# Context outputs of an S5 layer in quarters of TensorE, a later turn of the modulation, and other places for the first pages

## The chip, the core and the metric
One core of one Trainium2 chip. The metric is the device time of one launch, in microseconds (us). TensorE is called PE, VectorE DVE, ScalarE ACT, GpSimd POOL and SyncE SP, as in the profile; SP only issues DMAs here. TensorE's clock has two levels, 1.2 and 2.4 GHz; the profile gives it as a share of the upper one, so 0.50 is 1.2 GHz.

## What is computed
One inference step of a hybrid diffusion backbone, two layers deep: layer 0 mixes tokens with a bidirectional S5 state-space model, layer 1 with attention, and each is followed by a SwiGLU FFN. There are 256 context tokens and 1024 latent tokens of width 1024. All is fp32. The change lies in layer 0. Cut to what matters:

```python
def adaln(cvec, w_mod, b_mod):                  # the modulation
    m = jax.nn.silu(cvec) @ w_mod + b_mod
    return jnp.split(m[:, None, :], 6, axis=-1)

# s5_mixer: u = h @ w_in, 64 groups of 16 channels, each with a 64-dim complex state
...
s_re, s_im = scan(ab, bu)                       # per direction
y = einsum('blgp,ghp->blgh', s_re, c_re) - einsum('blgp,ghp->blgh', s_im, c_im)
...
z = jax.nn.gelu(y.reshape(b, l, D_MODEL))       # y also has d_skip * u
val, gate = jnp.split(z @ w_glu, 2, axis=-1)
return (val * jax.nn.sigmoid(gate)) @ w_out, finals
```

Context tokens and latent tokens go through the same mixer, each with its own modulation and its own initial states; the final states of the context are an output too.

## The kernel before
**Scan in blocks.** The S5 layer (`mixer0`) treats eight tokens as one block: 128 blocks for the latents, 32 for the context. The states at the block borders are found by a scan on DVE over two tiles X0 and X1 (32 groups of channels each; columns 0 to 128 hold the latents' states, 129 to 161 the context's). Inside a block, outputs come from tables: for each group a table of three 128x128 matrices multiplies the real part of the border states, their imaginary part, and the block's inputs U. The groups are handled in eight lots of eight (`fb`); the tables of a lot are one tile `tt` of 1.5 MB, loaded from DRAM (`s5_out_load`, L591, three buffers).

**Context outputs.** `ctx_items` (L636) yields the context's work in pieces. `states(fb)` copies a lot's border states out of X on ACT (L646, L647). `out(fb, h)` does half a lot: for each of four groups one matmul with the table's U part (L665) and two with its state parts (L667), the table as weights and 32 columns moving; a program-level fp32 matmul is two instructions. After the second half come a Gelu (L669), a store of the result to the DRAM buffer dZC on the POOL queue (L670), the load of the table three lots later, the states of two lots later, and `zload` of the lot before (L683, POOL queue), which brings dZC back turned into the tile zc. Then `net(t, h)` multiplies zc by the GLU weights (L698; loads L690 on SP), with a sigmoid or a copy on ACT (L704, L707), a product on POOL (L708) and a store (L709).

**Latents.** `s5_states` (L607) copies a lot's states, half on DVE (L614) and half on ACT (L617), or both on ACT (L616). `s5_out` (L620) has the same matmuls with 128 columns (L629, L631), a Gelu (L632) and a store of Z to dZL on POOL (L633). Between the latents' outputs stand pieces of `ctx_items`. Nine GLU products stand before the first latent output in the order of the program.

**Order.** In `mixer0` every engine runs its instructions as they are written. The function `drive` decides how the scan and the pieces are interleaved by a small clock of its own, from the number that each piece yields. Behind the mixer, in `rest`, only SP and POOL keep the written order; a planner places the instructions of PE, DVE and ACT. Memory pages are handed out in the written order of the program.

**Front of the FFN-like part.** `rest` starts with 16 page loads that bring dZL back turned (`zload` in `rest`, L1738 to L1742: two column chunks c, eight kt each), the splits into a high and a low part (L953 on ACT, L954 on DVE), and the weight loads and their splits (`i_load` L1028, `i_step` L1053, L1058, L1062). Products are L1100, 12 matmuls each. The pages used first lie over X1, whose last reader is the states of lot 7.

**Modulation.** 20 of the products of the conditioning with `w_mod` (`gemv`) are left; most are done in the mixer, the last 12 in `rest` by `gemv_next` (L201), once per piece of work: load four half pages (`hp`, L220, on ACT's queue), multiply a quarter that was loaded three calls earlier (L210), and after the fourth quarter copy the sum to a page (L214), turn it with four small products (L184, `gemv_tr`) and write it away (`gemv_fin`, L195, L196).

Of the kernel before, what the change touches and what calls it, by code (L numbers as in the profile page):

```python
# [6 lines left out]
F32 = mybir.dt.float32  # L7
F32R = mybir.dt.float32r
I32 = mybir.dt.int32
AF = mybir.ActivationFunctionType  # L10
# [3 lines left out]
P = 128  # L14
D = 1024
KT = 8
# [6 lines left out]
NG = 64  # L23
# [5 lines left out]
class Kernel:  # L29
# [171 lines left out]
    def gemv_next(self):  # L201

        nc = self.nc
        if len(self.gv) == 3 or not self.todo and self.gv:
            l, b, z, t = self.gv.pop(0)
            if z == 0:
                self.gp = self.psum()
            h, a = z // 2, z % 2
            for q in range(4):
                nc.tensor.matmul(self.gp[32 * q:32 * q + 32, 256 * h:256 * h + 256], self.sS[:, 4 * a + q, :], t[q],  # L210
                                 start=(a == 0), stop=(a == 1), tile_position=(0, 32 * q), skip_group_check=True)
            if z == 3:
                s = self.page()
                nc.scalar.activation(s, self.gp, AF.Copy)  # L214
                self.gemv_fin(l, b, self.gemv_tr(s))
        if self.todo:
            l, b, z = self.todo.pop(0)
            t = [self.half() for _ in range(4)]
            for q in range(4):
                nc.scalar.dma_start(t[q], self.I["w_mod"][l, b, :, 4 * (z % 2) + q, 256 * (z // 2):256 * (z // 2) + 256])  # L220
            self.gv.append((l, b, z, t))

# [9 lines left out]
class S5(Kernel):  # L232
# [355 lines left out]
                v.tensor_tensor(nxt, w[:, 0], w[:, 1], op=ALU.add)  # L588
                yield t + m * H / 960

    def s5_out_load(self, fb, ctx=False):  # L591

        nc = self.nc
        t = self.upool.tile([P, 8, 3, 128], F32, tag="tt", bufs=3, name=self.nm("tt"))
        nc.sync.dma_start(t, self.dW[:, fb])
        if ctx:
            U = [self.Uc[:, 8 * fb + k, :] for k in range(8)]
        else:

# [36 lines left out]
    def ctx_items(self):  # L636
# [2 lines left out]
        ld, W = [], []  # L639
        sc = {}  # L640

        def states(fb):
            X = self.X[fb // 4]
            gs = slice(8 * (fb % 4), 8 * (fb % 4) + 8)
            S = sc[fb] = sc["x"][:, fb % 2, 0:512].rearrange("p (g r c) -> p g r c", g=8, r=2)
            nc.scalar.activation(S[0:64], X[0:64, gs, :, 129:161], AF.Copy)  # L646
            nc.scalar.activation(S[64:128], X[64:128, gs, :, 160:128:-1], AF.Copy)  # L647

        def begin():
            ld.extend(self.s5_out_load(fb, True) for fb in range(3))  # L650
# [6 lines left out]
        def out(fb, h):  # L657
            U, t = ld[fb]
            if h == 0:
                sc["Z"] = sc["x"][:, fb % 2, 512:768]  # L660
                sc["ps"] = self.psum()
            ps = sc["ps"]
            for k in range(4 * h, 4 * h + 4):
                o = ps[:, 32 * k:32 * k + 32]
                nc.tensor.matmul(o, t[:, k, 2, :], U[k], start=True, stop=False)  # L665
                for ri in range(2):
                    nc.tensor.matmul(o, t[:, k, ri, :], sc[fb][:, k, ri, :], start=False, stop=(ri == 1))  # L667
            if h:
                nc.scalar.activation(sc["Z"], ps[:, 0:256], AF.Gelu_apprx_tanh)  # L669
                nc.gpsimd.dma_start(self.dZC[fb].rearrange("(p g) c -> p g c", g=8),  # L670
                                    sc["Z"].rearrange("p (g c) -> p g c", g=8))
                if fb < 5:
                    ld.append(self.s5_out_load(fb + 3, True))
                else:
                    self.ld.append(self.s5_out_load(fb - 5))
                if fb < 6:
                    states(fb + 2)
                if fb in (1, 3):
                    load()
                if fb:  # L680
                    zload(fb - 1)

        def zload(kt):  # L683
            nc.gpsimd.dma_start(self.zc[:, kt].rearrange("p (j c) -> p j c", j=8),
                                self.dZC[kt].rearrange("(j q) c -> q j c", j=8))
# [4 lines left out]
                nc.sync.dma_start(r, self.I["w_s5_glu"][len(W)])  # L690
                W.append(r)

        def net(t, h, ks=range(KT)):
            if ks[0] == 0:
                sc["ps", t, h] = self.psum()[:, 0:256]
            ps = sc["ps", t, h]
            for k in ks:
                nc.tensor.matmul(ps, W[2 * t + h][:, P * k:P * k + P], self.zc[:, k, :], start=(k == 0), stop=(k == KT - 1))  # L698
            if ks[-1] < KT - 1:
# [13 lines left out]
            for h in range(2):  # L713
                yield 2.6, lambda: out(fb, h)

        yield 2.6, lambda: net(0, 0, range(6))
        yield 3.5, lambda: (zload(7), net(0, 1, range(6)))
        for h in range(2):
            yield 0.9, lambda: net(0, h, range(6, 8))
        for t in range(1, 8):  # L720
            for h in range(2):
                yield 3.5, lambda: net(t, h)
# [937 lines left out]
class Full(Attn):  # L1660
# [40 lines left out]
    def rest(self):  # L1701
# [40 lines left out]
                                  self.dZL[kt].rearrange("(j q) c -> q j c", j=8)[:, 4 * c:4 * c + 4])  # L1742

        self.x_start(zz)
        for c in (0, 1):
            zload(c)
        self.x_all("B11", "B21")
        rest, k = self.x_rest("T1", "T2", "T3", "T4", "B22"), 0
        for c, units in self.ffn_heads(AF.Sigmoid):
            for u in units:  # L1750
                u()
                k += 1
                for _ in range(2 if k > 2 else 0):
                    next(rest, None)
                for _ in range(GN if k > GK else 0):
                    self.gemv_next()
        self.out_start(KT, TWO, self.spilled)
# [81 lines left out]
    def mixer0(self):  # L1839
# [182 lines left out]
        g, sm, tp = [self.gemv_load(*todo[0])], {}, {}  # L2022
        gk = [0]
        self.todo, self.gv = [(l, b, z) for l, b in todo[NGV:] for z in range(4)], []

        def gemv_step():
            k = gk[0]
# [209 lines left out]
```

## Time and profile before
| | us |
|---|---|
| median of 3 runs | 3416.73 |
| lowest and highest | 3413.44, 3417.08 |
| the profiled run | 3412.01 |
| its span, first to last instruction | 3410.2 |
| PE busy in it | 3254.1 (95%) |
| DVE busy | 2036.1 (60%) |
| ACT busy | 1390.3 (41%) |
| PE's share of the chain of waits that ended last | 76% |

The profile is that of one execution. The chain of waits is followed back from the last instruction, each step to what released it. "Idle before" is the time an engine sat idle ahead of an instruction, with what ended that idle time behind an arrow. PEld is the load of weights, which can run beside matmuls.

### The profile page before, as it was taken

What the parts mean: (1) busy time and instruction counts of PE and PEld (TensorE: products, weight loads), DVE (VectorE), ACT (ScalarE), POOL (GpSimd) and SP (SyncE); (2) the same over time, 40 slices, a digit from 0 to 9 for tenths busy, and PEclk for the clock granted to TensorE, in tenths of its full rate; (3) what the DMA queues carried; (4) which work ended last, traced back from release to release, by engine and by line L of the source; (5) the groups of instructions that cost most, each with busy time, mean ns of one, the idle gap of its engine ahead of it and who ended that gap; (6) DMA issues with size and microseconds to landing.
All of it is one profiled execution on the core that took longest, in us unless ns stands there. A gap on an engine that the chain in (4) does not pass through costs nothing.

```text
span 3410.2 us, 48179 instructions
## 1 busy us (share of the span) xinstructions
PE 3254.1 (95%) x18262; PEld 2759.6 (81%) x18262; DVE 2036.1 (60%) x4279; ACT 1390.3 (41%) x2714; POOL 287.6 (8%) x326
## 2 busy tenths in 40 slices
PE   8989979998999999999999999999889999999997
PEld 5768866677778888888788899999777888888787
DVE  8789716455574444443665788887557444444545
ACT  3261243243533222332544477775353322233433
POOL 2331100011000000001012310000100000000000
PEclk9996889999899999999999999999989999999998
DMA  7676675652231222343432200002123222235544
GB/s 257 177 227 237 209 251 183 192 201 74 86 102 66 69 67 73 118 150 106 145 115 76 68 24 11 14 27 75 68 88 98 69 70 72 69 105 192 173 127 146
DMA packets 204056, 398.81 MB, mean 117 GB/s; under 512 B 22624, under 2 KB 95616, under 8 KB 201520
## 3 DMA queue, kind: packets, MB, share of 16 engines
q1 hardware_dynamic: 154128, 322.52, 29.1%
q10 hardware_dynamic: 41040, 45.76, 4.0%
q0 software_dynamic: 8656, 27.45, 2.5%
q8 instruction: 143, 2.34, 0.3%
q14 instruction: 89, 0.73, 0.1%
HBM read 314.91 MB, written 84.93 MB: 117 GB/s over the span
## 4 chain that ended last, share of the span: by engine, by line
PE 76%; DVE 5%; ACT 3%; DMA 2%; issue 1%; ACTq 0%; SPq 0%; POOL 0%; DVEq 0%; POOLq 0%
PE ps L1100 29%; PE ps L121 9%; PE ps L123 8%; PE ps L125 8%; PE ps L1110 7%; PE ps L1549 2%; PE ps L1570 1%; PE ps L1569 1%; PE ps L1568 1%; PE ps L1507 1%; PE ps L1508 1%; PE ps L1509 1%; PE ps L829 1%; PE ps L210 1%; DVE pg L814 1%
## 5 line engine op out<-in xcount | busy, mean ns | idle before, releaser
L1100 PE MATMUL ps<-pg,pg 128*128 128x512 f32 x4368 | 1053.6, 399 | 35.3 <-ACT pg L1058 20.7
L1100 PEld LDWEIGHTS ps<-pg,pg 128*128 128x128 f32 x4368 | 826.1, 192 | 228.5 <-ACT pg L1058 22.1
L121 PE MATMUL ps<-pg,pg 128*128 128x512 f32 (+1 forms) x1872 | 633.7, 363 | 18.7 <-ACT pg L102 7.3
L125 PE MATMUL ps<-pg,pg 128*128 128x512 f32 (+1 forms) x1872 | 625.9, 358 | 5.1 <-DVE pg L103 5.1
L123 PE MATMUL ps<-pg,pg 128*128 128x512 f32 (+1 forms) x1872 | 628.2, 359 | 0.3
L121 PEld LDWEIGHTS ps<-pg,pg 128*128 128x128 f32 x1872 | 347.2, 191 | 80.7 <-ACT pg L102 9.4
L125 PEld LDWEIGHTS ps<-pg,pg 128*128 128x128 f32 x1872 | 346.8, 190 | 60.8 <-DVE pg L103 8.5
L123 PEld LDWEIGHTS ps<-pg,pg 128*128 128x128 f32 x1872 | 347.5, 191 | 55.0 <-DVE pg L132 1.5
L103 DVE TENSOR_TENSOR pg<-wr,pg 128x512 fp32r<-128x512 f32 (+1 forms) x312 | 218.5, 729 | 196.2 <-ACT pg L102 123.6
L1110 PEld LDWEIGHTS ps<-pg,pg 128*128 128x128 f32 x2112 | 271.7, 196 | 21.5 <-DVE pg L1062 8.5
L1110 PE MATMUL ps<-pg,pg 128*128 128x256 f32 x2112 | 276.7, 288 | 12.4 <-DVE pg L1062 7.2
L102 ACT ACTIVATE pg<-wr 128x512 fp32r<-128x512 f32 (+1 forms) x312 | 175.5, 596 | 270.8 <-DMA wr<-in_w_ffn_out 90.9
L1062 DVE TENSOR_TENSOR pg<-pg,pg 128x512 fp32r<-128x512 f32 x208 | 142.6, 687 | 138.6 <-ACT pg L1058 132.0
L1062 DVE TENSOR_TENSOR pg<-wr,pg 128x512 fp32r<-128x512 f32 x214 | 145.7, 686 | 92.9 <-ACT pg L1058 92.2
L1058 ACT ACTIVATE pg<-pg 128x512 fp32r<-128x512 f32 x208 | 126.9, 628 | 147.7 <-PE ps L1100 42.2
L132 DVE TENSOR_TENSOR pg<-ps,pg 128x512 fp32r<-128x512 f32 (+1 forms) x210 | 141.8, 676 | 57.9 <-ACT pg L131 52.4
L1058 ACT ACTIVATE pg<-wr 128x512 fp32r<-128x512 f32 x214 | 128.7, 624 | 74.5 <-PE ps L1110 33.6
L1529 ACT ACTIVATE pg<-ps,nb,rq 128x512 f32<-128x512 f32 x192 | 148.8, 776 | 5.4 <-DVE sm L1538 2.4
L131 ACT ACTIVATE pg<-ps 128x512 fp32r<-128x512 f32 (+1 forms) x210 | 123.4, 589 | 64.6 <-PE ps L1549 47.9
L747 DVE SCALAR_TENSOR_TENSOR pg<-ps,mods,pg 128x512 f32<-128x512 f32 x64 | 47.9, 749 | 159.4 <-PE ps L125 154.7
L1279 POOL TENSOR_TENSOR pg<-pg,pg 128x512 f32<-128x512 f32 x8 | 10.7, 1335 | 1540.2 <-DVE pg L747 862.8
L1514 DVE TENSOR_REDUCE mx<-ps 128x1 f32<-128x512 f32 (+1 forms) x208 | 136.9, 660 | 1.3 <-PE ps L1509 1.3
(359 smaller groups left out, 4727.6 us busy)
## 6 DMA issues: line engine op xcount, KB each, us to landing
wr<-in_w_ffn_in SPq DMA_DIRECT2D x104, 512.0 KB, 3.5
wr<-in_w_ffn_out SPq DMA_DIRECT2D x80, 512.0 KB, 4.2
dI<-pg SPq DMA_DIRECT2D x104, 256.0 KB, 2.0
pg<-dI SPq DMA_DIRECT2D x104, 256.0 KB, 4.9
gw<-in_w_mod SPq DMA_DIRECT2D x96, 256.0 KB, 5.2
tt<-dW SPq DMA_DIRECT2D x16, 1536.0 KB, 6.9
hp<-in_w_mod ACTq DMA_DIRECT2D x192, 128.0 KB, 2.4
wr<-in_w_s_glu SPq DMA_DIRECT2D x37, 512.0 KB, 4.6
```

What stands on the lines that cost most here:

```text
L102: nc.scalar.activation(hi, x, AF.Copy)
L103: nc.vector.tensor_tensor(lo, x, hi.bitcast(F32), op=ALU.subtract)
L121: mm(ps[c], wh, rh[c], start=first, stop=False)
L123: mm(ps[c], wh, rl[c], start=False, stop=False)
L125: mm(ps[c], wl, rh[c], start=False, stop=last)
L132: self.nc.vector.tensor_tensor(lo, src, hi.bitcast(F32), op=ALU.subtract)
L1058: nc.scalar.activation(hi, self.isum[i, name], AF.Copy)
L1062: v.tensor_tensor(lo, self.isum[i, name], hi.bitcast(F32), op=ALU.subtract)
L1100: mm(e[bank], p[:, o], q, start=(first and k == 0 and j == 0), stop=(k == 3 and j == 2), skip_group_check=True)
L1110: mm(ps, p[:, o], q, start=(k == 0 and j == 0), stop=(k == KT - 1 and j == 2))
L1514: v.tensor_reduce(mx[:, kc:kc + 1], ps, axis=AX.X, op=ALU.max)
L1529: nc.scalar.activation(p, u["bank"].pop((qt, kc)), AF.Exp, bias=nb[:, 0:1], scale=rq, accum_out=sm[:, kc:kc + 1])
```

## The change
Four edits, all in the S5 layer and the start of what follows it:

1. **Context outputs.** In `out`, the states and U become the weights (128x32) and the table moves (128 columns); the four groups of a half lie in four quarters of 32 columns of the array. The result has tokens and channels the other way round, so ACT copies it to a tile `y` (128x128), PE transposes it, and ACT does the Gelu. This `turn` of one half is written behind the matmuls of the next half. The lots come in the order 3, 4, 5, 6, 7, 0, 1, 2, so that the tables of lots 0, 1 and 2 are the last three; they stay in SBUF and serve the first three lots of the latents, whose loads (three of 1.5 MB) go.
2. **Turn of the modulation.** `gemv_next` puts the copied page aside (`self.gt`), and the turn and `gemv_fin` come at the start of the next call.
3. **Gate on modulation loads.** In the first three calls, each of the 12 half-page loads is preceded by an ACT copy of one column from the last page of the 16 page loads (`zz[7][1]`) into the half page, so that the load can't be before that page has landed.
4. **Memory and order at the start of `rest`.** X1 is allocated below X0 instead of above it, so that the pages and half pages that are used first lie over X0. One page is taken by a memset of one column on POOL. The splits of the first column chunk (B11) are written ahead of the page loads of the second.

```diff
     def gemv_next(self):
         nc = self.nc
+        if self.gt:
+            l, b, s = self.gt.pop()
+            self.gemv_fin(l, b, self.gemv_tr(s))
...
                 nc.scalar.activation(s, self.gp, AF.Copy)
-                self.gemv_fin(l, b, self.gemv_tr(s))
+                self.gt.append((l, b, s))
...
             for q in range(4):
+                if self.gz is not None:
+                    nc.scalar.activation(t[q][:, 0:1], self.gz[:, 0:1], AF.Copy)
                 nc.scalar.dma_start(t[q], self.I["w_mod"][l, b, :, 4 * (z % 2) + q, 256 * (z // 2):256 * (z // 2) + 256])
...
-    def s5_out_load(self, fb, ctx=False):
+    def s5_out_load(self, fb, ctx=False, t=None):
-        t = self.upool.tile([P, 8, 3, 128], F32, tag="tt", bufs=3, name=self.nm("tt"))
-        nc.sync.dma_start(t, self.dW[:, fb])
+        if t is None:
+            t = self.upool.tile([P, 8, 3, 128], F32, tag="tt", bufs=3, name=self.nm("tt"))
+            nc.sync.dma_start(t, self.dW[:, fb])
...
+        ORD = (3, 4, 5, 6, 7, 0, 1, 2)
...
-            for k in range(4 * h, 4 * h + 4):
-                o = ps[:, 32 * k:32 * k + 32]
-                nc.tensor.matmul(o, t[:, k, 2, :], U[k], start=True, stop=False)
-                for ri in range(2):
-                    nc.tensor.matmul(o, t[:, k, ri, :], sc[fb][:, k, ri, :], start=False, stop=(ri == 1))
+        def turn():
+            if "y" in sc:
+                i, h, y = sc.pop("y")
+                ps = self.psum()[:, 0:128]
+                nc.tensor.transpose(ps, y, self.ident)
+                Z = sc["x"][:, i % 2, 512:768]
+                nc.scalar.activation(Z[:, 128 * h:128 * h + 128], ps, AF.Gelu_apprx_tanh)
+                if h:
+                    nc.gpsimd.dma_start(self.dZC[ORD[i]].rearrange("(p g) c -> p g c", g=8), Z.rearrange("p (g c) -> p g c", g=8))
+        def out(i, h):
+            U, t = ld[i]
+            ps = self.psum()[:, 0:128]
+            for j in range(3):
+                for q in range(4):
+                    k = 4 * h + q
+                    nc.tensor.matmul(ps[32 * q:32 * q + 32], U[k] if j == 2 else sc[i][:, k, j, :], t[:, k, j, :],
+                                     start=(j == 0), stop=(j == 2), tile_position=(0, 32 * q), skip_group_check=True)
+            y = self.upool.tile([P, 256], F32, tag="gg", bufs=2, name=self.nm("gy"))[:, 0:128]
+            nc.scalar.activation(y, ps, AF.Copy)
+            turn()
+            sc["y"] = i, h, y
...
-                    self.ld.append(self.s5_out_load(fb - 5))
+                    self.ld.append(self.s5_out_load(ORD[i], t=t))
...
-        for c in (0, 1):
-            zload(c)
-        self.x_all("B11", "B21")
+        nc.gpsimd.memset(self.page()[:, 0:1], 0.0)
+        zload(0)
+        self.x_all("B11")
+        zload(1)
+        self.x_all("B21")
...
+                self.gz = zz[7][1] if k < GK + 4 else None
...
-        self.X = [xpool.tile([P, NG // 2, 2, 162], F32, name=f"X{i}") for i in range(2)]
+        self.X = [xpool.tile([P, NG // 2, 2, 162], F32, name=f"X{i}") for i in (1, 0)][::-1]
```

## Rows read from the trace of the kernel before
**Rows 1.** Stages: length, busy PE PEld DVE ACT POOL, clock, DMA share, GB/s.

```profile
330.00:365.00 35.00, 35.00 (x153) 33.92 (x153) 35.00 (x201) 4.57 (x8) 5.61 (x8) 0.50 0.67 231
```

**Rows 2.** Groups by line on PE, 276 to 402: busy, mean ns, idle before.

```profile
L667 PE MATMUL ps<-scx,tt 128*128 128x32 f32 x256 | 66.6, 401 | 0.0
```

**Rows 3.** PE in order of time: start, length, line; 276 to 476.

```profile
277.67 0.60 PE L665 MATMUL ps<-Uc,tt 128*128 128x32 f32 x2 [1.48 <-DMA tt<-dW]
...
359.58 9.04 PE L698 MATMUL ps<-zc,wr 128*128 128x256 f32 x26
...
374.58 19.82 PE L698 MATMUL ps<-zc,wr 128*128 128x256 f32 x80 [2.91 <-DMA wr<-in_w_s_glu]
...
402.06 0.38 PE L629 MATMUL ps<-ul,tt 128*128 128x128 f32 x2
...
475.52 0.61 PE L631 MATMUL ps<-S,tt 128*128 128x128 f32 x4
```

**Rows 4.** DVE in order of time, where the scan of X0 ends.

```profile
371.75 0.28 DVE L576 TENSOR_TENSOR X<-sw 128x64 f32<-128x64 f32 x1
...
372.27 0.81 DVE L576 TENSOR_TENSOR X<-sw 128x64 f32<-128x64 f32 x1
...
376.30 1.21 DVE L614 COPY S<-X 64x2048 f32<-64x2048 f32 x1
```

**Rows 5.** ACT in order of time, the states of the first latent lot.

```profile
394.91 1.91 ACT L617 ACTIVATE S<-X 64x2048 f32<-64x2048 f32 x1
```

**Rows 6.** PE in order of time, products behind the mixer, and at one turn.

```profile
492.31 4.34 PE L1100 MATMUL ps<-pg,pg 128*128 128x512 f32 x12 [16.18 <-ACT pg L1058]
500.31 5.87 PE L1100 MATMUL ps<-pg,pg 128*128 128x512 f32 x14 [3.65 <-ACT pg L1058]
...
581.61 1.05 PE L184 MATMUL ps<-sel,pg 128*128 128x2 f32 x8 [1.05 <-ACT pg L214]
582.53 4.30 PE L1100 MATMUL ps<-pg,pg 128*128 128x512 f32 x12
...
587.57 3.03 PE L1100 MATMUL ps<-pg,pg 128*128 128x512 f32 x12
```

**Rows 7.** ACT in order of time, behind the mixer's end.

```profile
476.25 9.88 ACTq L220 DMA_DIRECT2D hp<-in_w_mod  x12
486.17 3.23 ACT L953 ACTIVATE pg<-pg 128x512 fp32r<-128x512 f32 x6 [9.41 <-DMA hp<-in_w_mod]
```

**Rows 8.** SP in order of time, page loads and weight loads.

```profile
470.36 23.26 SPq L1741 DMA_DIRECT2D pg<-dZL  x16
493.66 1.78 SPq L1028 DMA_DIRECT2D wr<-in_w_s_glu  x3
```

**Rows 9.** Table by stage, the stretch between mixer and first product.

```profile
476.00:493.00 17.00, 0.82 (x4) 0.50 (x2) 5.62 (x10) 6.12 (x11) 0.53 (x1) 0.66 0.93 263
```

**Rows 10.** PE's waits, 470 to 705: in total, times, longest.

```profile
PE ps L184 <- ACT pg L214: 6.6, 5, 1.6
```

**Rows 11.** PE in order of time, a stretch of four column groups abreast.

```profile
149.71 0.70 PE L440 MATMUL ps<-to,BBd 128*32 128x144 f32 x16
```

**Rows 12.** A float transpose on PE: ns min/median/max.

```profile
L535 PE MATMUL ps<-ident,ti x128: 272/273/476, 163.4 to 238.2; 128*128 128x128 f32 x128
```

**Rows 13.** DMA issues, 260 to 500: count, KB each, us to landing.

```profile
dZC<-scx POOLq DMA_DIRECT2D x8, 128.0 KB, 6.2
zc<-dZC POOLq DMA_DIRECT2D x8, 128.0 KB, 6.7
```

**Rows 14.** DMA issues of 476 to 500, the same columns.

```profile
pg<-dZL SPq DMA_DIRECT2D x13, 256.0 KB, 5.4
...
wr<-in_w_s_glu SPq DMA_DIRECT2D x3, 512.0 KB, 6.2
dZL<-Z POOLq DMA_DIRECT2D x1, 512.0 KB, 3.2
```

**Rows 15.** SP's waits, 500 to 720: in total, times, longest.

```profile
SPq L1028 <- DVE pg L1053: 54.2, 7, 16.8
```

More of the change, by code (lines that the diff above doesn't have):

```diff
@@ L640, in ctx_items, with states @@
         sc = {}
-        def states(fb):
+        def states(k):
+            fb = ORD[k]
             X = self.X[fb // 4]
             gs = slice(8 * (fb % 4), 8 * (fb % 4) + 8)
-            S = sc[fb] = sc["x"][:, fb % 2, 0:512].rearrange("p (g r c) -> p g r c", g=8, r=2)
+            S = sc[k] = sc["x"][:, k % 2, 0:512].rearrange("p (g r c) -> p g r c", g=8, r=2)
             nc.scalar.activation(S[0:64], X[0:64, gs, :, 129:161], AF.Copy)
             nc.scalar.activation(S[64:128], X[64:128, gs, :, 160:128:-1], AF.Copy)
+        ORD = (3, 4, 5, 6, 7, 0, 1, 2)
         def begin():
-            ld.extend(self.s5_out_load(fb, True) for fb in range(3))
+            ld.extend(self.s5_out_load(fb, True) for fb in ORD[:3])
             sc["x"] = self.prmo.tile([P, 2, 768], F32, tag="PO", name="scx")
@@ L655, in begin @@
             states(1)
[L657 to L662, printed above, removed]
-            for k in range(4 * h, 4 * h + 4):
-                o = ps[:, 32 * k:32 * k + 32]
-                nc.tensor.matmul(o, t[:, k, 2, :], U[k], start=True, stop=False)
-                for ri in range(2):
-                    nc.tensor.matmul(o, t[:, k, ri, :], sc[fb][:, k, ri, :], start=False, stop=(ri == 1))
-            if h:
[L669 to L673, printed above, removed]
-                else:
-                    self.ld.append(self.s5_out_load(fb - 5))
-                if fb < 6:
-                    states(fb + 2)
-                if fb in (1, 3):
+        def turn():
[7 more added lines that the diff above has]
+                    nc.gpsimd.dma_start(self.dZC[ORD[i]].rearrange("(p g) c -> p g c", g=8), Z.rearrange("p (g c) -> p g c", g=8))
@@ new lines, in out @@
+        def out(i, h):
[10 more added lines that the diff above has]
+            sc["y"] = i, h, y
+            if h:
+                if i < 5:
+                    ld.append(self.s5_out_load(ORD[i + 3], True))
+                else:
+                    self.ld.append(self.s5_out_load(ORD[i], t=t))
+                if i < 6:
+                    states(i + 2)
+                if i in (1, 3):
@@ L679, in out @@
                     load()
-                if fb:
-                    zload(fb - 1)
+            elif i > 1:
+                zload(ORD[i - 2])
         def zload(kt):
@@ L691, in load, with net @@
                 W.append(r)
-        def net(t, h, ks=range(KT)):
-            if ks[0] == 0:
+        def net(t, h, ks=ORD):
+            if ks[0] == ORD[0]:
                 sc["ps", t, h] = self.psum()[:, 0:256]
@@ L697, in net @@
             for k in ks:
-                nc.tensor.matmul(ps, W[2 * t + h][:, P * k:P * k + P], self.zc[:, k, :], start=(k == 0), stop=(k == KT - 1))
-            if ks[-1] < KT - 1:
+                nc.tensor.matmul(ps, W[2 * t + h][:, P * k:P * k + P], self.zc[:, k, :], start=(k == ORD[0]), stop=(k == ORD[-1]))
+            if len(ks) == 6:
                 return
@@ L714, in ctx_items @@
                 yield 2.6, lambda: out(fb, h)
-        yield 2.6, lambda: net(0, 0, range(6))
-        yield 3.5, lambda: (zload(7), net(0, 1, range(6)))
+        yield 2.6, lambda: (turn(), zload(ORD[6]), net(0, 0, ORD[:6]))
+        yield 3.5, lambda: (zload(ORD[7]), net(0, 1, ORD[:6]))
         for h in range(2):
-            yield 0.9, lambda: net(0, h, range(6, 8))
+            yield 0.9, lambda: net(0, h, ORD[6:])
         for t in range(1, 8):
@@ L2024, in mixer0 @@
         self.todo, self.gv = [(l, b, z) for l, b in todo[NGV:] for z in range(4)], []
+        self.gt = []
         def gemv_step():
```

## The prediction
> **What bounds the kernel now.** I read the table by stage first, because the chain of waits gives PE three quarters of the span and does not say where PE is slow. From 330 to 365 us PE is busy for the whole window at a granted clock of 0.50, its lower level of 1.2 GHz, and DVE is just as full, with the scan [rows 1]. The groups by line show what fills PE: matmuls of 32 columns in the context's outputs, 401 ns each, 256 instructions on the line of the states alone [rows 2]. PE in order of time shows them from 277.67 to 359.58 us, then the context's GLU products (L698) until the latents' first output at 402.06, and the mixer's last matmul, which ends at 475.52 + 0.61 = 476.13 [rows 3]. Call that end E. From the first latent output on, PE has 74.1 us of work and small waits, so what counts is when that output may start. It needs its turn on PE (402.06) and its states: the X0 scan ends at 376.30 with the copy on DVE [rows 4], and ACT's half of the copy takes 1.91 us, only at 394.91 [rows 5], because it is written behind the evacuation of the seventh GLU product. So PE sets the start; the states could be ready some 22 us earlier.
>
> Behind E comes a hole. PE's first FFN product starts at 492.31, 16.18 us after E, and PE waits again for 3.65 us before 500.31 [rows 6]. On ACT, 12 loads of modulation halves take 9.88 us of issue, and the first split (L953) follows at 486.17 [rows 7]; on SP the 16 page loads are in issue from 470.36 for 23.26 us, so that the weights (L1028) go out at 493.66 [rows 8]. The DMA engines are nearly full in that hole, at a share of 0.93 and 263 GB/s [rows 9]. Later, in the FFN, the modulation's turn (L184) makes PE wait for the copy L214 five times, 6.6 us in all [rows 10].
>
> **Context's outputs.** A half of a group of eight has 12 matmuls of two instructions each. Its 24 instructions now move 128 columns and go four abreast. The same shape of work is L440: 16 instructions (128x32 weights, 144 columns) in 0.70 us [rows 11]. 24 of them are 24/16 x 0.70 = 1.05 us, and 2.1 at half clock. Added are one copy and one short Gelu on ACT, which is busy 4.57 of 35 us there [rows 1], and a float transpose of two instructions like L535, 273 ns each [rows 12]. PE's bill for a group of two halves is 2 x (1.05 + 0.55) = 3.2 us warm and 6.4 at half clock, against (359.58 - 277.67)/8 = 10.2 now. Bounds: if the four abreast did not overlap, 48 instructions at the transpose's 273 ns and twice that for the clock would be 26 us, far slower than now; if they overlap and no copy is waited for, 3.2. I take the concurrent value, since L440 shows it on this chip.
> Then the table loads set the pace: 1.57 MB at the 263 GB/s of the full stretch [rows 9] is 6.0 us. The first is there at 277.67, the eighth at 277.67 + 7 x 6.0 = 319.7, and the last outputs, with their turn, are done near 325 instead of 359.6. The three tables that are kept spare loads only behind this stage, beside PE's work, and are costed at nothing.
> The last zc needs a store of 6.2 us and a load of 6.7 [rows 13], so the first two GLU products are done near 340. Seven more took 402.06 - 374.58 = 27.5 us with their waits for weights [rows 3]: 367.5. Now the scan is last. Three more GpSimd multiplies fall beside it, and each stretches one DVE instruction as at 372.27, from 0.28 to 0.81 us [rows 4]: 1.5 us. The states are ready at 376.3 + 1.5 + 1.9 = 379.7, which is 22.3 us before 402.06. PE will have idled for some 12 us and restart at the lower level: after its 16.18 us of idle 12 products took 4.34 us where 12 warm ones take 3.03, and the next 14 took 5.87 for 3.5 [rows 6]. That is 3.7 at most; I take 3. **Gain 19 us**, between 12 (GLU products at half clock, 7 x 7 = 49 us, would end at 389) and 22. Behind the start the order is as before, so the 74.1 us stay.
> The Trainium skill, SBUF — State Buffer, section "Who interferes with whom", says that a DVE instruction with two SBUF inputs contends with a GpSimd instruction that reads SBUF; the stretched row at 372.27 agrees. The Trainium skill, TensorE: Matmul & The Clock Gate, Part 4, says that transposes do not count for the clock as other PE work does; no row of before shows it for this stage, and by it the GLU products would begin slow, as at the lower end.
>
> **Front of the FFN.** First, the first pages and halves lie over X0, which is free long before X1 (read by the states until the eighth group), and a page load waits for its page at the head of SP's queue; now only the Z stores hold them. The last store is issued near E + 0.9 and lands in 3.2 us, a page load takes 5.4 [rows 14], then come a split on ACT (0.6) and its DVE half (0.7): E + 11.8 at the latest, less as the 12 modulation loads no longer share the engines. I take E + 9.5 for the first product, against E + 16.2. Second, the weights follow eight further page loads at some 0.82 us each (ACT's 9.88/12), from about E + 4.6: issue near E + 11.3, landing 6.2 [rows 14], split 1.3: the second product starts near E + 18.8 against E + 24.2. Third, zload(1) behind the splits of B11 costs SP nothing: SP has issues only, and the splits are on ACT and DVE. Fourth, the 12 modulation loads are gated by tiny copies that wait for the last page of zload(1). The queue on which they wait is ACT's: 12 x (0.82 + 0.2) = 12 us, and behind them stand whatever splits and L1058 the planner puts there. If that is L1058 of the second product, it goes at about E + 16 + 12 = E + 28, a loss of 4. If not, the gain is 5.4, and up to 9 with faster landings. No row decides; I take **4**, from -4 to +9. The memset is hidden: POOL runs one instruction in the whole hole [rows 9].
>
> **Modulation's turn.** The turn moves one call later, behind a product of 12 matmuls (3.03 us), which hides the 0.6 us copy. Removed are 6.6 us of wait, and what follows: after the wait at 581.61 the next 12 take 4.30 us against 3.03 [rows 6], so four such cost 5.1. The page and the PSUM tile are held one call longer. **Gain 11**, from 4 (most of the wait comes back, for modulation halves) to 14.
>
> Sum: 19 + 4 + 11 = 34. From the profiled run's 3412.0 this gives 3378; from the median of 3416.7, 3382.7. The profiled run lies 1.4 us under the fastest timed one, so I predict 3380, between them.
>
> **Rivals.** R1, the gate blocks ACT: L1058 of the second product, and of more steps, stand behind the 12 copies and issues. For it: 9.88 us of issue stands ahead of L953 now [rows 7]. Against: the planner may place products first. The front loses 4 instead of winning 4, and the turns give 2 less: 3390. The Trainium skill, Trainium Kernel Development and Optimization, Key Constraints, says that all queues share 16 engines and the choice of queue saves only issue time; the share of 0.93 agrees, and speaks for later modulation loads.
> R2, E moves less: tables, weights and ul loads keep a pace near 10 us, or the GLU products run cold. For it: half clock through the stage [rows 1]. E gains 6: 3393.
> R3, the change does not do what it says: the planner sets the turn right behind its copy again, and the waits stay: 3391.
> R4, more of everything: front 9, turns 14, E 22 and no cold restart: 3369.
> R5, **slower**: the page that holds the copied sum lives one call longer, and pages are handed out in the order of the program; when the ring comes round, the load or split that reuses it waits, and SP's weights (L1028) with it. Place: 12 turns. Price: up to a product of 12 each, 3.03 to 4.30 us. With 23 us won by the rest, the kernel is slower from 2 us a turn. For it: L1028 waits 54.2 us for pages that DVE reads in the sums of weights (L1053) [rows 15]. Against: those waits are hidden, and a ring is longer than a call. At 3.5 us: 42 - 23 = 19 slower, 3434.
>
> **How the numbers follow.** Forecast 0.42 (3370 to 3388 by itself), R1 0.20, R2 0.12, R3 0.10, R4 0.10, R5 0.06. The range leaves out R5, a part of R4 and the far end of R2: 3357 to 3404. A change of 0.2% (6.8 us) is about what a measurement of this kernel can tell from none. Faster: all but R5 and the tail of R2, 0.89; same 0.05; slower 0.06.
>
> **What would show it.** Right: a group of context outputs under 7 us, with PE waiting for tt; PE idle before the first L629, waiting for S; that start at 378 to 384; E near 457; the first L1100 under 11 us after E; no PE wait for L214. Wrong: L629's start still set by L698 (R2), ACT's 12 issues ahead of the second L1058 (R1), L184 straight behind L214 (R3), SP waiting for a page that L184 reads (R5).

## The result and the profile after

| | us |
|---|---|
| before, median of 4 runs (lowest to highest) | 3416.27 (3413.44 to 3417.08) |
| changed, median of 4 runs | 3373.82 (3372.48 to 3376.83) |
| ratio, 95% interval | 0.9878 (0.9861 to 0.9896) |
| profiled run of the changed kernel, its span | 3374.14, 3372.1 |

The change takes 42.5 us off the median (forecast: 34 by the sum, 36.7 from the median to the 3380 predicted). Between the two profiled spans it is 38.1 us. Line numbers have moved: L687 is the quartered output, L674 its turn, L720 the GLU product, L637 and L639 the latents' outputs, L975 and L1080 the first splits and L1122 the FFN products.

The stage of [rows 1] again, in the same window and the one ahead of it, with the same columns: PE, which had been full at half clock, is busy for 14.8 of 30 and 28.1 of 35 us, at 0.67 and 0.82. DVE is as full as before.

```profile
300.00:330.00 30.00, 14.80 (x250) 9.62 (x250) 30.00 (x158) 12.26 (x30) 4.06 (x6) 0.67 0.55 207
330.00:365.00 35.00, 28.06 (x182) 20.94 (x182) 35.00 (x195) 8.72 (x23) 10.38 (x14) 0.82 0.61 207
```

The groups by line on PE, 276 to 382 us (busy, mean ns, idle before): the states' and the inputs' parts of the outputs, two lines before [rows 2], are one line now and take 14.0 + 8.7 us of PE, and the turns 6.7, for a stage of 82 us before. What is new is idle time ahead of the turn.

```profile
L687 PE MATMUL ps<-tt,scx 128*32 128x128 f32 x256 | 14.0, 355 | 3.4 <-DMA tt<-dW 2.0 <-ACT scx L656 1.5
L687 PE MATMUL ps<-tt,Uc 128*32 128x128 f32 x128 | 8.7, 354 | 0.0
L674 PE MATMUL ps<-ident,gy 128*128 128x128 f32 x16 | 6.7, 421 | 35.0 <-ACT gy L690 35.0
```

PE in order of time, beside [rows 3] and [rows 6]:

```profile
280.10 0.64 PE L687 MATMUL ps<-tt,scx 128*32 128x128 f32 x16 [1.47 <-ACT scx L656]
280.56 0.40 PE L687 MATMUL ps<-tt,Uc 128*32 128x128 f32 x8
...
308.79 0.48 PE L674 MATMUL ps<-ident,gy 128*128 128x128 f32 x1 [26.70 <-ACT gy L690]
...
340.28 0.98 PE L674 MATMUL ps<-ident,gy 128*128 128x128 f32 x2
...
352.45 16.33 PE L720 MATMUL ps<-zc,wr 128*128 128x256 f32 x64 [2.72 <-DMA wr<-in_w_s_glu]
...
380.50 0.38 PE L637 MATMUL ps<-ul,tt 128*128 128x128 f32 x2
...
452.51 0.61 PE L639 MATMUL ps<-S,tt 128*128 128x128 f32 x4
461.77 4.66 PE L1122 MATMUL ps<-pg,pg 128*128 128x512 f32 x12 [8.65 <-ACT pg L1080]
470.38 2.50 PE L1122 MATMUL ps<-pg,pg 128*128 128x512 f32 x5 [3.95 <-ACT pg L1080]
```

The first lot starts at 280.10, and then PE waits 26.7 us; the outputs end near 341 (359.6 before), the first latent output starts at 380.50 (402.06), and the mixer ends at 452.51 + 0.61 = 453.12 (476.13). The first FFN product comes 8.65 us behind the end (16.18), the second wait is 3.95 (3.65). The long wait is explained by ACT's waits, 276 to 382 us (total, times, longest): the copy of the second lot's context states waits for the scan's step on X1, and three Gelus wait for a store of dZC.

```profile
ACT scx L655 <- DVE X L583: 27.1, 1, 27.1
...
ACT scx L676 <- DMA dZC<-scx: 10.2, 3, 5.2
```

ACT in order of time, beside [rows 5] and [rows 7]: the latents' first states are copied at 377.03, after which they and the GLU products (PE, above) are ready almost together. Behind the mixer the splits start at once; the eighth waits for its page, and behind the weight splits of the first product stand the gate's first copies, which wait 6.14 us for the last page; the second product's split comes after them and waits 0.93 us more, for its weights.

```profile
377.03 1.91 ACT L625 ACTIVATE S<-X 64x2048 f32<-64x2048 f32 x1 [3.34 <-DVE X L583]
...
453.78 3.75 ACT L975 ACTIVATE pg<-pg 128x512 fp32r<-128x512 f32 x7
460.57 0.63 ACT L975 ACTIVATE pg<-pg 128x512 fp32r<-128x512 f32 x1 [3.04 <-DMA pg<-dZL]
461.11 1.13 ACT L1080 ACTIVATE pg<-wr 128x512 fp32r<-128x512 f32 x2
468.38 0.39 ACT L226 ACTIVATE hp<-pg 128x1 f32<-128x1 f32 x3 [6.14 <-DMA pg<-dZL]
...
469.70 0.63 ACT L1080 ACTIVATE pg<-wr 128x512 fp32r<-128x512 f32 x1 [0.93 <-DMA wr<-in_w_s_glu]
```

A turn in the FFN, PE in order of time (compare 581.61 to 587.57 in [rows 6]): no wait, 0.95 us, and the next 12 products take 3.02 us.

```profile
552.65 0.95 PE L184 MATMUL ps<-sel,pg 128*128 128x2 f32 x8
553.53 0.64 PE L214 MATMUL ps<-hp,sS 128*32 128x256 f32 x8
554.10 3.02 PE L1122 MATMUL ps<-pg,pg 128*128 128x512 f32 x12
```

Where the 38.1 us of the two spans lie, as the lead of the changed kernel at the same instruction in both traces: -2.4 us at the first context output, +21.6 at the first latent output, +23.0 at the mixer's end, +30.5 at the first FFN product, +31.2 after 120 of its matmuls, +43.7 after 640, +39.6 after 900, +38.1 at the end. So mixer 23.0, hole and the first products 8.2, turns 12.4, and 5.5 given back afterwards. The cut at 120 matmuls gives the turns too little: the first of the five waits of [rows 10], 1.20 us at 534.27, lies ahead of it, and with the later turn alone (below) the lead grows by 3.1 us from the first product to there. Moved over, that leaves about 5.1 us for the hole and 15.5 for the turns, an estimate. The -2.4 at the start is not explained: the first context output starts at 276.0 to 277.8 us in the four profiles without edit 1 and at 277.8 to 281.4 in the ten with it. Counted from that instruction, the mixer gains 25.4 us.

### The profile page after: what moved, and what is told of

It is laid out like the page before. It is cut to its first block, busy times and chain, and to the rows that moved or that the text cites. A ratio compares the mean times of both kernels' runs of the same rounds, so it can differ in the third digit from the quotient of the medians.

```text
span 3372.1 us, 48270 instructions
## 1 busy us (share of the span) xinstructions
PE 3191.4 (95%) x18278; PEld 2692.7 (80%) x18278; DVE 2036.3 (60%) x4279; ACT 1396.2 (41%) x2750; POOL 288.2 (9%) x327
## 4 chain that ended last, share of the span: by engine, by line
PE 77%; DVE 5%; ACT 2%; issue 1%; DMA 1%; SPq 0%; ACTq 0%; POOL 0%; DVEq 0%; POOLq 0%
PE ps L1122 29%; PE ps L121 9%; PE ps L123 9%; PE ps L125 9%; PE ps L1132 7%; PE ps L1571 2%; PE ps L1592 1%; PE ps L1591 1%; PE ps L1590 1%; PE ps L1529 1%; PE ps L1530 1%; PE ps L1531 1%; PE ps L851 1%; PE ps L214 1%; DVE pg L836 1%
## 5 line engine op out<-in xcount | busy, mean ns | idle before, releaser
L1122 PE MATMUL ps<-pg,pg 128*128 128x512 f32 x4368 | 1047.3, 397 | 28.4 <-ACT pg L1080 13.4
L1122 PEld LDWEIGHTS ps<-pg,pg 128*128 128x128 f32 x4368 | 824.1, 191 | 222.1 <-issue 15.8
L1080 ACT ACTIVATE pg<-pg 128x512 fp32r<-128x512 f32 x208 | 127.3, 628 | 149.3 <-DVE pg L1084 40.3
L1080 ACT ACTIVATE pg<-wr 128x512 fp32r<-128x512 f32 x214 | 128.7, 624 | 68.7 <-PE ps L1132 33.6
```

Source lines behind the costliest of these rows:

```text
L1080: nc.scalar.activation(hi, self.isum[i, name], AF.Copy)
L1122: mm(e[bank], p[:, o], q, start=(first and k == 0 and j == 0), stop=(k == 3 and j == 2), skip_group_check=True)
```

## The experiments

Each run's total is told against the kernel before on the same chip. These medians of before lay between 3412.5 and 3416.3, so a difference of two or three microseconds between kernels with different such medians is not read from totals; places in the trace are told against the mixer's end E instead, which is the start of the first FFN product less its idle time. The first three experiments and the gate alone put parts of the change's own diff on the kernel before; the diffs of the others are against the changed kernel.

**The context's outputs alone.** Edit 1 of the change and nothing else.

> The kernel before with the context outputs' edit alone (quarters, turn, order of lots, kept tables). Theory: this part alone moves the mixer's end, and the hole behind it and the modulation's waits stay as they were. The last L631-type matmul ends near 453 us instead of 476 (in the changed kernel it ended at 453.1), PE waits some 16 us for its first product and 6.6 us for the turns; total 21 to 25 us below the kernel before, near 3393. Rival: the mixer's gain needs the other places of X0 and X1 or the kept order of loads, or part of it is eaten by the hole (page loads wait for X1 anyway): end at 453, but a longer wait for the first product, total only 10 to 15 below.

Measured 3387.26 against 3413.19: 25.9 us less (ratio 0.9922, 0.9907 to 0.9937). PE in order of time, and PE's waits, 440 to 720 us:

```profile
468.84 5.07 PE L1122 MATMUL ps<-pg,pg 128*128 128x512 f32 x12 [14.13 <-ACT pg L1080]
```

```profile
PE ps L184 <- ACT pg L218: 4.9, 5, 1.6
```

E is 468.84 - 14.13 = 454.71, 21.4 us earlier than before; the hole (14.13 us instead of 16.18) and the turns' waits (4.9 instead of 6.6) stay nearly as they were. The gain of the mixer stands alone, a little above the 21 to 25 us expected, and nothing of it is eaten in the hole.

**The later turn alone.** Edit 2.

> The kernel before with the later turn of the modulation alone. Theory: the waits of PE for the copied page (6.6 us) go, and the half-clock stretches behind four of them as well: 11 to 13 us below the kernel before, near 3404, with no PE wait for that copy and the 12 products behind a turn at 3.0 instead of 4.3 us. Rival: the clock falls for another reason (the turn's own small matmuls): only 5 to 7 us below. Second rival: the planner moves the turn but a page or the GLU's mods wait for it: within 3 us of before.

Measured 3402.32 against 3413.19: 10.9 less (0.9961, 0.9948 to 0.9974). PE in order of time at a turn:

```profile
577.34 0.95 PE L184 MATMUL ps<-sel,pg 128*128 128x2 f32 x8
...
578.79 3.02 PE L1107 MATMUL ps<-pg,pg 128*128 128x512 f32 x12
```

The table by stage, first of the kernel before behind its turn at 581.61, then of this run around the turn above (length, busy times, granted clock, DMA share, GB/s):

```profile
582.50:586.80 4.30, 4.30 (x18) 2.94 (x20) 1.21 (x5) 1.33 (x3) 0.20 (x1) 0.66 0.44 150
```

```profile
577.30:581.80 4.50, 4.50 (x33) 3.26 (x36) 3.02 (x8) 1.33 (x3) 0.31 (x1) 1.00 0.75 200
```

No turn waits, and the 12 products behind this one are at 3.02 us instead of 4.30 [rows 6], with the same eight small matmuls of the turn ahead of them. The granted clock behind the turn that waited was 0.66, and 1.00 through the one that did not, as through all eleven turns of this run from 532 to 694 us. So the turn's own work does not bring the lower level. Nor does every wait: behind the fourth of the five in the kernel before the products keep the pace of the full clock.

```profile
649.65 1.05 PE L184 MATMUL ps<-sel,pg 128*128 128x2 f32 x8 [1.19 <-ACT pg L214]
650.57 2.06 PE L1100 MATMUL ps<-pg,pg 128*128 128x512 f32 x8
```

From the 120th to the 640th matmul of the products the kernel gains 12.9 us. Four of the five waits lie there, 5.4 us of the 6.6 [rows 10]. Behind three of them the granted clock was at its lower level, 0.50, from 583.9 to 587.3, from 601.0 to 604.4 and from 696.5 to 700.0 us; half of these 10.3 us, some 5.1, is what the lower level cost, an estimate. What the remaining 2.4 us are is not shown.

**The front alone.** Edits 3 and 4.

> The kernel before with the front's edits alone: gate on 12 modulation loads, X0 and X1 exchanged, the dummy page and the order of page loads. Theory: the mixer's end stays at 476 and the first product starts 8 to 9 us behind it instead of 16.2; total 7 to 9 below the kernel before, near 3408. Rival: the gain of the hole in the changed kernel came from the mixer (X1's states are read earlier against the end there): here the first product starts 12 or more behind the end, and the total is within 4 of before.

Measured 3408.1 against 3413.19: 5.1 less (0.9989, 0.9979 to 0.9998). PE in order of time:

```profile
481.83 5.23 PE L1107 MATMUL ps<-pg,pg 128*128 128x512 f32 x12 [9.33 <-ACT pg L1065]
```

The hole is 9.3 instead of 16.2 without any help of the mixer. The total gained less than the 7 to 9 expected; the lead after 120 matmuls is 3.2 us smaller than at the first product. The three parts alone give 25.9 + 10.9 + 5.1 = 41.9 us, against 42.5 for the whole change: they add up, as far as totals with intervals of 3 to 5 us to either side can tell.

**Without the gate.**
```diff
-                self.gz = zz[7][1] if k < GK + 4 else None
+                self.gz = None
```

> The changed kernel without the gate: the 12 modulation loads are issued as soon as their half pages are free. Theory: the loads share the DMA engines with the last page loads and take ACT's time ahead of the splits, so the first product starts 11 to 14 us behind the mixer's end instead of 8.65: total 3 to 6 above the changed kernel. Rival: with the half pages over X0 the loads go during the mixer, before the page loads, and the gate buys nothing: first product at 8 to 9, total within 1.5 of the changed kernel, or below it, as the 12 small copies and waits on ACT are gone.

Measured 3377.2 against 3413.19, 36.0 less. ACT in order of time, then PE:

```profile
455.67 9.24 ACTq L227 DMA_DIRECT2D hp<-in_w_mod  x12
464.95 4.49 ACT L975 ACTIVATE pg<-pg 128x512 fp32r<-128x512 f32 x8 [8.70 <-DMA hp<-in_w_mod]
```

```profile
470.01 5.23 PE L1122 MATMUL ps<-pg,pg 128*128 128x512 f32 x12 [14.39 <-ACT pg L1080]
```

The hole is back at 14.39 us, a little past the 11 to 14 of the theory: the 12 issues take 9.24 us of ACT's queue, and the splits wait behind them. That is as without any of the front's edits (14.13 above). Of the front, then, the places in memory and the order of page loads do nothing without the gate.

**The same loads, ungated, on GpSimd's queue.**
```diff
-                if self.gz is not None:
-                    nc.scalar.activation(t[q][:, 0:1], self.gz[:, 0:1], AF.Copy)
-                nc.scalar.dma_start(t[q], self.I["w_mod"]...
+                (nc.gpsimd if self.gz else nc.scalar).dma_start(t[q], self.I["w_mod"]...
...
+                self.gz = k < GK + 4
```

> The changed kernel with no gate, and with the first 12 modulation loads issued on GpSimd's queue instead of ACT's. Theory 1, the gate helps because it takes 9 us of issue off ACT's queue ahead of the first splits: the first product starts 8.5 to 10 us behind the mixer's end, though the loads run at the same time as the page loads; total within 2 of the changed kernel. Theory 2, it helps because the loads don't share the DMA engines with the page loads: the first product starts 12 to 14.5 us behind the end, as without the gate (14.39); total 3 to 5 above the changed kernel.

Measured 3374.84 against 3412.66, 37.8 less. ACT, then PE, in order of time:

```profile
452.92 3.85 ACT L972 ACTIVATE pg<-pg 128x512 fp32r<-128x512 f32 x7
464.10 0.63 ACT L972 ACTIVATE pg<-pg 128x512 fp32r<-128x512 f32 x1 [7.33 <-DMA pg<-dZL]
```

```profile
465.30 5.49 PE L1119 MATMUL ps<-pg,pg 128*128 128x512 f32 x12 [13.05 <-ACT pg L1077]
```

The page loads, 440 to 480 us (count, KB each, us from issue to landing), first of the changed kernel, then of this run:

```profile
pg<-dZL SPq DMA_DIRECT2D x14, 256.0 KB, 5.0
pg<-dZL SPq DMA_DIRECT2D x14, 256.0 KB, 6.5
```

Now ACT is free and splits seven pages at once, but the eighth page lands late: ACT waits 7.33 us for it, where the gated kernel waited 3.04, and page loads take 6.5 us to land instead of 5.0. The hole is 13.05. So the sharing of the DMA engines costs 4.4 us here with no issue on ACT. From ACT's queue, with both, it was 5.7; the two lie over each other, and what the issue time would cost by itself is not separated. The totals of this run and the changed kernel can't be told apart, though the second theory had 3 to 5 us between them.

**The gate alone** (edit 3 on the kernel before; X0, X1 and page loads as before).

> The kernel before with the gate on the first 12 modulation loads alone; X0, X1 and the order of page loads as before. Theory, the gate is the whole of the front's gain, since it keeps 12 loads from sharing the DMA engines with the last page loads: first product 8 to 10.5 us behind the mixer's end instead of 16.2, total 4 to 8 below the kernel before, as with all of the front's edits (5.1 below). Rival, the gate needs the other places: its loads' half pages or the page loads wait for X1, first product 12 or more behind the end, total within 3 of the kernel before.

Measured 3411.96 against 3412.46: no change (1.0, 0.999 to 1.0009). ACT, then PE, in order of time:

```profile
491.41 0.30 ACT L226 ACTIVATE hp<-pg 128x1 f32<-128x1 f32 x2 [13.26 <-DMA pg<-dZL]
491.62 0.61 ACT L960 ACTIVATE pg<-pg 128x512 fp32r<-128x512 f32 x1
```

```profile
494.03 9.27 PE L1107 MATMUL ps<-pg,pg 128*128 128x512 f32 x29 [19.68 <-ACT pg L1065]
```

Neither expectation: the hole is longer than before, 19.68. With both chunks' page loads written ahead of the splits, the planner puts the first two gate copies ahead of three splits of the first chunk, and these wait 13.26 us with them for the last page. The second wait of the kernel before is gone, though (29 matmuls run in one row), so that the longer hole costs nothing in the end: the lead on the kernel before is 1.8 us at E and 1.6 after 120 matmuls. The gate pays only with edit 4 beside it. That it is the splits, written ahead of the second chunk's loads, is argued from these rows; the page taken by the memset came and went with that order in every run here and was not tried by itself.

**X0 and X1 in their old places**, all else as changed.
```diff
-        self.X = [... for i in (1, 0)][::-1]
+        self.X = [... for i in range(2)]
```

> The changed kernel with X0 and X1 in their old places, so that the first pages and half pages lie over X1 again, which the latents' states read until the eighth lot; gate and order of page loads stay. Theory, the hole is set by the last store of Z and by which loads share the engines, and the last page loads can't start before that store anyway: first product 8 to 11 us behind the mixer's end, total within 2 of the changed kernel. Rival, the pages' places are half of the gain: page loads start when the eighth lot's states are copied (some 8 us before the end) and those pages that need no late store come too late; first product 12 or more behind the end, total 3 to 6 above.

Measured 3373.06 against 3414.73, 41.7 less. PE in order of time:

```profile
461.50 4.94 PE L1122 MATMUL ps<-pg,pg 128*128 128x512 f32 x12 [8.26 <-ACT pg L1080]
```

The hole is 8.26. The exchange of X0 and X1, in which the prediction saw the first reason for a shorter hole, moves nothing that these runs can see.

**Lots in natural order, tables loaded again.**
```diff
-        ORD = (3, 4, 5, 6, 7, 0, 1, 2)
+        ORD = (0, 1, 2, 3, 4, 5, 6, 7)
-                    self.ld.append(self.s5_out_load(ORD[i], t=t))
+                    self.ld.append(self.s5_out_load(i - 5))
```

> The changed kernel with the lots in the order 0 to 7 and all eight tables loaded again for the latents. The second lot then lies in X0, so the 26.7 us wait of the second lot for X1's context states (DVE, to 307) moves to the fifth lot, and four lots lie before it. Theory, the scan of X0 and the GLU products nearly tie at the first latent output (states ready at 378.9, products done at 380.5): the context outputs end 8 to 15 us earlier than 340, and the first latent output starts at 379 to 383 all the same, now released by the states; total within 2 of the changed kernel. Rival, the context's chain sets that start alone: it moves by 8 or more with the outputs, to 372 or less. Second rival: three more table loads cost the tail, total 3 or more above.

Measured 3374.94 against 3412.66, 37.7 less. PE in order of time, then ACT:

```profile
309.52 0.48 PE L674 MATMUL ps<-ident,gy 128*128 128x128 f32 x1 [17.85 <-ACT gy L690]
...
329.47 1.22 PE L720 MATMUL ps<-zc,wr 128*128 128x256 f32 x2 [4.07 <-DMA zc<-dZC]
...
380.08 1.20 PE L639 MATMUL ps<-S,tt 128*128 128x128 f32 x4 [5.71 <-ACT gu L729]
```

```profile
377.66 1.91 ACT L625 ACTIVATE S<-X 64x2048 f32<-64x2048 f32 x1 [11.21 <-DVE X L583]
```

The wait for X1's states is 17.85 us and lies behind four lots, and the outputs end 18 us earlier than in the changed kernel. The first latent output's part with U, which needs no states, starts at 373.99; then PE waits 5.71 us for the states, which ACT copies until 379.57 and DVE until 379.94. The tie is shown: with the outputs out of the way the scan sets the start, and nothing is gained (E is 454.77, against 453.12). That the tables of three lots are loaded again does not show in the total either; order and loads were changed together here, and what the loads cost by themselves was not tried.

**Four buffers for the Gelu's output.**
```diff
-                Z = sc["x"][:, i % 2, 512:768]
+                if h == 0:
+                    sc["Z"] = self.upool.tile([P, 256], F32, tag="zb", bufs=4, name=self.nm("zb"))
+                Z = sc["Z"]
```

> The changed kernel with four buffers for the context's Gelu output instead of two, so that a Gelu doesn't wait for the store of two lots earlier (waits of 3.05, 5.15 and 1.98 us on ACT in the changed kernel). Theory, the same tie: the outputs end 6 to 10 us earlier (331 to 335), the first latent output still starts at 379 to 382; total within 2 of the changed kernel. Rival, the outputs' chain is bounded by table loads instead: they end at 337 or later. Second rival: start and total move by the full 6 to 10.

Measured 3372.62 against 3412.66, 40.0 less. PE in order of time:

```profile
327.61 1.08 PE L689 MATMUL ps<-tt,scx 128*32 128x128 f32 x16 [4.33 <-DMA tt<-dW]
...
338.80 1.08 PE L689 MATMUL ps<-tt,scx 128*32 128x128 f32 x16 [2.69 <-DMA tt<-dW]
```

The first rival: the waits for the store are gone, and four waits for tables stand in their place, 4.33 and 2.69 us the longest; the outputs end no earlier.

**Every quartered matmul twice.**
```diff
-            for j in range(3):
+            for j in range(3 + 3):
+                j %= 3
```

> The changed kernel with every context matmul of the quartered outputs done twice in a row (the first set is written over by the second). Theory, the stage is set by X1's context states (to 307), then by table loads and stores, and PE has room: each half costs 1.1 to 1.7 us more, the outputs end 3 to 10 us later than 340, and the first latent output and the end slip by at most 8; total 0 to 8 above the changed kernel. Rival, PE sets the stage behind 307: 14 halves at 1.7 us more, outputs end 24 us later, total 15 to 24 above.

Measured 3376.89 against 3414.73, 37.8 less. PE's waits, 276 to 460 us:

```profile
PE ps L674 <- ACT gy L691: 25.2, 2, 24.9
PE ps L688 <- DMA tt<-dW: 8.2, 4, 2.6
```

PE's busy time on these matmuls grows from 22.7 to 40.8 us, and the outputs end 6.5 us later than in the changed kernel (346.85) and the first latent output 5.7 us later (386.16). PE still waits for states and tables; the form of the matmuls has room to spare, but the tie leaves no slack behind it.

**More GLU products ahead of the first latent output.** The natural order above, and:
```diff
-                yield 2.6, lambda: out(fb, h)
+                yield 1.6, lambda: out(fb, h)
```
The smaller number makes `drive` write the context's pieces earlier: 13 products instead of 9 stand ahead of the first latent output. One run has the four Gelu buffers as well, one has not.

> The changed kernel with both of the others' edits (lots in natural order, four Gelu buffers) and the context outputs yielded at 1.6 instead of 2.6, which writes 13 GLU products ahead of the first latent output instead of 9. If the scan of X0 is what sets that start once the outputs end earlier, four products of 3.5 us move from behind the start to the idle time of PE before it: start at 379 to 384, the mixer's end 8 to 14 us earlier than 453, total 3360 to 3367. Rival: weight loads of the GLU (3.9 us a product) do not let 13 products be done by 380, the start slips to 385 to 392 and the gain is under 4. Second rival: the tail then waits for tables or for X1's states, and the end stays within 4 of 453.

> The changed kernel with lots in natural order and 13 GLU products ahead of the first latent output, but with two Gelu buffers as in the changed kernel. Theory, with four lots before X1's states come the stores of Gelu outputs are not waited for: mixer's end at 442 to 446 and a total of 3362 to 3368, as with four buffers (3364.8). Rival, the four buffers carry part of that gain: end at 447 or later, total 3369 or more.

Measured 3364.77 against 3412.66 (0.9861, 0.9846 to 0.9875) with four buffers, and 3364.66 against 3414.73 (0.9853, 0.9836 to 0.9869) without. Both beat the changed kernel, by some 9 us by their medians. PE in order of time, without the buffers:

```profile
344.84 24.86 PE L720 MATMUL ps<-zc,wr 128*128 128x256 f32 x96 [2.76 <-DMA wr<-in_w_s_glu]
370.21 7.14 PE L720 MATMUL ps<-zc,wr 128*128 128x256 f32 x32 [0.51 <-ACT gu L729]
...
385.25 3.69 PE L720 MATMUL ps<-zc,wr 128*128 128x256 f32 x16 [0.19 <-DMA wr<-in_w_s_glu]
...
423.35 0.71 PE L639 MATMUL ps<-S,tt 128*128 128x128 f32 x4 [2.39 <-ACT S L625]
...
454.18 5.49 PE L1122 MATMUL ps<-pg,pg 128*128 128x512 f32 x12 [9.31 <-ACT pg L1080]
```

From 344.84 on PE hardly waits. The latents start later (388.77, and 387.14 with the buffers) and not at the 379 to 384 expected, but with four products fewer behind them; E is 454.18 - 9.31 = 444.87, 8.3 us earlier than with the changed kernel. The buffers carry nothing that the totals show.

## Why the prediction was right, and where it was not

**The mixer: 23.0 us, forecast 19.** Right in its main step: the outputs leave PE's path and the scan's states come level with it. The start of the latents at 380.50 agrees with the 379.7 of the sum. But that it agrees so well is partly luck: the steps ahead of it, which were to end at 367.5, well before the states, took until 380.5. The pace of the outputs was put at the table loads, with an end near 325; they ended at 341, since the second lot needs X1's context states, which the scan gives at 307 (wait of 27.1 us), and then Gelus wait for stores and, without these, for tables. I had read the order of lots as a matter of tables only, and not which part of the scan each lot reads. So the GLU products ended at 380.5: PE set the start after all, level with the states (copied by 378.94 on ACT and 379.31 on DVE). Of the signs that the prediction named for being right, PE waiting for tables hardly came (2.0 us in all) and PE idle for S ahead of the latents not at all; the one that it named for R2, a start still set by the GLU products, did, though E came earlier than forecast and not later. And as the GLU products ran into the latents with no idle time between, the 3 us for a restart at the lower clock, which the sum took off the start, did not fall due there. That is most of the 4 us by which this term was too small; the rest is the part behind the start, 72.6 us instead of 74.1. The three more GpSimd multiplies beside the scan became two in the trace, at 0.80 us each.
The abreast form was priced a little high: the 24 instructions of the first half of L687 run from 280.10 to 280.96, 0.86 us against the 1.05 worked out from [rows 11]. So was the transpose, which is one instruction here and not two: 16 of L674 for 16 halves. PE was at half clock for much of the stage again, and doubling its work cost only 6 us.

**The hole: 7.5 us at the first product, about 5 after 120 matmuls, forecast 4.** The first product came at E + 8.65 (forecast 9.5), the second at E + 17.3 (18.8). The size was near, the reason was partly wrong. The exchange of X0 and X1 does nothing (8.26 without it); the gate is what counts, and only beside the order of page loads that the sum had costed at nothing: alone it makes the hole 19.68. R1, ACT blocked behind the gate, did not come in the changed kernel, where the copies wait 6.14 us ahead of the second product's split but end 0.93 us before its weights land; it did come in the gate alone, in the form that splits of the first chunk were caught.

**The turn: 12.4 us, and some 3 more ahead of the 120th matmul, forecast 11.** Right in both terms, the wait and the half clock behind it, and too small in size by the traces. The waits are the 6.6 us of the sum. The half clock, 5.1 in the sum, is nearer 6.8: half of the 10.3 us behind three of the waits, and half of the 3.3 us by which the stretch at 0.50 around the first wait (532.7 to 539.5) is longer than that of the kernel with the later turn (528.1 to 531.6). Some 2 us of the 15.5 stay open. Totals can't decide: the interval of the later turn alone is 8.9 to 17.7 us. R3 and R5 fell: no turn waits, and no wait of SP for a page that a turn reads is seen.

**Given back.** Between the 640th and the 900th matmul the changed kernel loses 4.1 us of its lead. Its profile shows one wait of 2.15 us for ACT at 693.61 and slower matmuls behind it, at a granted clock of 0.50 from 694.0 to 697.4. Eight of the experiments' kernels with edits 1 and 2 lose 0.5 to 1.7 us there, so most of it belongs to that run; why the rest comes was not tried.

The total lies 6 us below the predicted one and inside the range. Between the profiled runs the terms were short by 4.0 (mixer), about 1.1 (hole) and about 4.5 (turn), and 5.5 were given back, which the sum did not have: 34 + 9.6 - 5.5 = 38.1. The other 4.4 to the medians' 42.5 lie in the profiled run of before, which was 4.3 us faster than its median; I had put 3380 halfway for that.

## What to carry to other kernels

When a stage on one engine is made three times cheaper, the next bound can be a near tie of several chains, and then removing any one of them buys nothing; the gain comes from moving other work into the idle time, as writing four more products ahead of the scan's end did here (9 us). Ask of every reordering not only which loads it saves but which producer each piece waits for, in time. A gate on early loads must stand behind everything that does not need the gated data in the order of its engine, or it becomes the wait that it was meant to remove.

## What was not expected of the hardware

Twelve loads of 128 KB beside the last page loads lengthen the hole by 4.4 us even from a queue that nothing waits on (13.05 from GpSimd's, 8.65 gated). And a wait of only 1.05 to 1.56 us ahead of a turn can be followed by the lower clock: three such waits in the kernel before were, and the slow products behind them cost some 1.7 us a time (an estimate, a third of the 5.1 us above), more than the wait. It is no rule: a wait of 1.19 us at 649.65 was not followed by it, nor, with the context's outputs alone, one of 1.56 us at 579.16, behind which 12 products took 3.02 us. What decides it is not shown. The Trainium skill, TensorE: Matmul & The Clock Gate, Part 4, says that transposes do not count for the clock as other work does. In the changed kernel the stage with its turns ran at 0.67 and 0.82, partly at the lower level, but it was idle for long stretches too, so no run here tells the two apart.
